# Two parts of the conditioning vectors of a two-block network: row sums on VectorE or products on TensorE

## The chip, the cores and the metric

One NeuronCore of a Trainium2 chip runs the whole program. Its engines each work through their own queue in order: TensorE (PE, with its weight loads PEld), VectorE (DVE), ScalarE (ACT), GpSimd (POOL), and SyncE (SP), which here only issues transfers. The metric is the device time of one execution in microseconds.

## What is computed

Two blocks follow each other on x of 256 x 1024 (float32). The first has two layers: attention with a rotary part, then a state-space mixer, each followed by a feed-forward layer. Each of its four sublayers is modulated by the vector c (1 x 1024):

```python
cs = jax.nn.silu(c)
shift, scale, gate = modulation(cs, w, b)     # split(cs @ w + b, 3), w: 1024 x 3072
h = x * (1.0 + scale) + shift
x = layer_norm(ALPHA * x + (1.0 + gate) * y, g, b)
```

So every sublayer needs three thirds of a vector-matrix product: shift, scale and gate. The second block (recurrent mixer, attention with a bias, gated feed-forward layers) has no modulation and is not touched.

## The kernel before

**Weights.** All weights lie in memory as units of 128 x 1024 float32 (512 KB), in the order in which `plan()` lists them. `_issue` loads them through SP into a ring of seven tiles `raw`. `run` processes units: a weight unit ("w") is split into `wh` (ACT, L464, rounded to fp32r) and `wl` (DVE, L504, the rest) in one of eleven slots, and TensorE then makes three fp32r products for one exact one; a modulation unit ("m") goes to `mod_unit`. A raw tile is loaded anew when the unit in it has been processed, so SP's queue waits on the engines that read the ring.

**Modulation.** `modIT` is third T (0 shift, 1 scale, 2 gate) of sublayer I; it has eight units. A unit holds 128 columns of the weight, turned, so that a partition holds one column. `mod_unit` (L542) multiplies it on DVE by `cs` (silu(c) copied to all partitions) and sums along the row: one `scalar_tensor_tensor` of 128 x 1024 with a sum (L555), which leaves 128 numbers as a column. Shift and scale are wanted as columns (`mcol`), the gate as a full tile: `mod_finish` spreads the column over 128 rows by eight products with the identity and copies them into `GATE` on ACT (L581).

**The stage of the change.** `mla()` is the first attention. After the key and value products it loops over eight heads in `heads`, in an order that a string sets; a letter is a step of the head so many iterations back, a number is `run` for so many units, `q` makes the queries of the next two heads:

```python
HEADS0 = "T2 S0 B0 1 A2 E0 1 N0 q 1"
```

S is the scores (PE; four float32 products and two that add the mask), B the row maxima (DVE), E the exponentials (ACT), N the division by the row sum (DVE reciprocal, ACT), T the turning of the probabilities (PE, copied by ACT, L1095), A the product with the values (PE) and its split (ACT L636, DVE L637). The three `1` take one unit each, so that an iteration also takes one unit of `mla_o`, the output weight, and two modulation units. In `plan()` these are `mod11` (the scale of the first feed-forward layer) and then `mod02` (the gate of the attention itself); the first two units of `mod11` come ahead of the heads. Behind the heads `need_mod("mod02")` calls `mod_finish`, and `boundary("mla_o", ...)` makes the output product, first for the upper 128 rows of x, then for the lower ones. `norm(0)` is the layer norm of the upper half. `make_xt(0)` then modulates the turned upper half and splits it into `XH` (ACT) and `XL` (DVE, L637), and `f_pass` starts the feed-forward product `mlp0.f` with it.

**The tables.** POOL makes four tables of rotations (`rot`) during the heads; they lie in what becomes slots 9 and 10 of the weight ring. `put_tables` (L1440) sends them to memory and marks "tables" as finished; until then `run` can't use these two slots (`self.lent`). In the kernel before it stands directly behind the heads.

Of the kernel before, what the change touches and what calls it, by code (L numbers as in the profile page):

```python
# [11 lines left out]
F32 = mybir.dt.float32  # L12
F32R = mybir.dt.float32r
I32 = mybir.dt.int32
AF = mybir.ActivationFunctionType
# [37 lines left out]

def _mod(i, third):
    return [("m", "mod%d%d" % (i, third), k) for k in range(8)]
# [67 lines left out]
def _unit(inp, kind, tag, k, out):  # L123
# [5 lines left out]

    if kind == "m":  # L130
        i, third = int(tag[3]), int(tag[4])
        nm, l = _MOD[i]
        o = 1024 * third + 128 * k
        out[:] = inp[nm + "_w"][l][:, o:o + 128].T
        return
# [62 lines left out]
def _cols_spec():  # L198
    s = [("dsk", lambda i: i["ssm_d"][0])]
# [44 lines left out]
for _u in UNITS:  # L244
    WPOS.append(WPOS[-1] + (_u[0] == "w"))
    RPOS.append(RPOS[-1] + (_u[0] in "mwx"))
RUNITS = [_j for _j, _u in enumerate(UNITS) if _u[0] in "mwx"]
# [65 lines left out]
class Model:  # L313
    def __init__(self, ctx, tc, ws, cols, rows, x, pos, inv, rel, sp, sbc, sgb, out):
# [33 lines left out]
        self.mhalf = T("mhalf", [128, 4])  # L348
        self.one = T("one", [128, 1])
# [81 lines left out]
    def run(self, look=LOOK, maxn=99, mods=2):  # L431
        n = 0
        while self.nproc < len(UNITS) and n < maxn:
# [4 lines left out]
            if u[0] == "m":  # L438
                if mods == 0 or (self.hold and self.modfin is not None and u[1][4] == '2'):
                    break  # L440
                mods -= 1
# [31 lines left out]
            elif u[0] == "m":  # L473
                self.mod_unit(u, raw)
            elif u[0] == "x":
                self.kept[u] = raw
# [93 lines left out]

    def mod_finish(self):
        if self.modfin is None:
            return
        self.mods.add(self.modfin[0])
        self.modfin = None
        for n in range(2):
            b = self.bank()
            for m in range(4):
                self.mm(b[:, 128 * m:128 * m + 128], self.gcol[:, 4 * n + m:4 * n + m + 1].to_broadcast([128, 128]),
                        self.ident, True, True)  # L580
            self.nc.scalar.activation(self.GATE[:, 512 * n:512 * n + 512], b, func=AF.Copy)  # L581
            self.rel(b)
# [399 lines left out]
    def setup(self):  # L982
# [32 lines left out]
        self.rel(*cb)  # L1015
        self.ssm_decay(spt, pi)
# [93 lines left out]
    def mla(self):  # L1110
# [130 lines left out]
        self.put_tables()  # L1241
# [4 lines left out]
        def norm(h):  # L1246
            if h == 0:
                self.ssm_tables()
                self.halves()
            if h == 1:  # L1250
                self.load_row(self.GR, "ln_mix_g0")
                self.load_row(self.BR, "ln_mix_b0")
            self.ln_part(h, accs[h], ALPHA)
# [850 lines left out]
```

## Time and profile before

| | |
|---|---|
| time, median of 3 runs | 1689.81 us (1685.68 to 1692.23) |
| the profiled execution | 1692.64 us, of it 1690.9 us span |
| mean granted TensorE clock | 0.969 |
| busy over the span | PE 94%, DVE 67%, ACT 50%, POOL 14% |

A span is from the first to the last instruction of the profiled execution, and all times inside it are counted from its start. Busy shares are means over stages that differ: the heads lie between 51 and 124 us, the output product behind them until 148 us. In the views "<-" behind an instruction's idle time names what ended it. PEclk is the granted TensorE clock as a share of 2.4 GHz, so 0.50 is 1.2 GHz. One float32 product appears as two records with two weight loads, one fp32r product as one.

### The profile page before, as it was taken

The numbers are of one execution on the slowest core, as the hardware profiler recorded it, in microseconds if no ns is written. First come the engines' busy times: TensorE is split into PE (matmuls) and PEld (weight loads), VectorE is DVE, ScalarE is ACT, GpSimd is POOL, SyncE is SP. The second block draws the span as 40 slices with busy tenths as digits, with TensorE's granted clock in tenths as the row PEclk, the third lists the DMA queues.
The fourth block names the chain that finished last, engine by engine and source line by source line (L and its number), as shares of the span: only waits on it lengthen the run. The fifth ranks groups of instructions, "written<-read, shape, count | busy, mean of one in ns | idle before, by whom it ended". The sixth has DMA issues, their size and how long they took to land.

```text
span 1690.9 us, 24901 instructions
## 1 busy us (share of the span) xinstructions
PE 1589.7 (94%) x9594; PEld 1400.8 (83%) x9594; DVE 1130.8 (67%) x1568; ACT 838.4 (50%) x1285; POOL 238.5 (14%) x309
## 2 busy tenths in 40 slices
PE   6779999998789999999999889999999999999998
PEld 2558888987778899789997768999899998779997
DVE  7777887779977745767554777555755555775553
ACT  3454567746355655354434745444644444654341
POOL 7990000013523000100000020000000001330000
PEclk8879999998889999999999989999999999999999
DMA  9774788967466566475541547565555663545540
GB/s 367 285 246 157 256 300 295 345 228 294 165 225 244 216 221 206 140 254 198 203 170 47 178 175 260 176 236 174 189 179 189 217 209 103 187 153 203 205 150 26
DMA packets 106586, 349.62 MB, mean 207 GB/s; under 512 B 12385, under 2 KB 22753, under 8 KB 106466
## 3 DMA queue, kind: packets, MB, share of 16 engines
q1 hardware_dynamic: 106466, 348.02, 58.6%
q8 instruction: 75, 1.23, 0.3%
q14 instruction: 45, 0.37, 0.1%
HBM read 338.41 MB, written 9.57 MB: 206 GB/s over the span
## 4 chain that ended last, share of the span: by engine, by line
PE 49%; DVE 4%; ACT 3%; issue 1%; POOL 1%; DMA 0%; DVEq 0%; POOLq 0%; ACTq 0%
PE bank L400 48%; ACT junka L693 1%; DVE wl L504 1%; PE bank L644 1%; ACT wh L464 0%; DMA raw<-in_ws_dram 0%; DVE r L731 0%; ACT r L1870 0%; POOL wl L468 0%; DVE z L1844 0%; ACT z L1871 0%; POOL st L689 0%; DVE z L1300 0%; DVE z L1903 0%; DVE st L1284 0%
## 5 line engine op out<-in xcount | busy, mean ns | idle before, releaser
L504 DVE TENSOR_TENSOR wl<-raw,wh 128x1024 fp32r<-128x1024 f32 x448 | 538.8, 1236 | 161.9 <-ACT wh L464 159.9
L464 ACT ACTIVATE wh<-raw 128x1024 fp32r<-128x1024 f32 x464 | 471.6, 1051 | 246.1 <-PE bank L400 131.8
L400 PE MATMUL bank<-xh,wh 128*128 128x256 f32 x1664 | 469.3, 282 | 0.0
L400 PE MATMUL bank<-xh,wl 128*128 128x256 f32 x1664 | 468.4, 282 | 0.0
L400 PE MATMUL bank<-xl,wh 128*128 128x256 f32 x1664 | 468.3, 281 | 0.0
L400 PEld LDWEIGHTS bank<-xh,wh 128*128 128x128 f32 x1664 | 317.0, 190 | 2.7 <-DVE z L1651 0.2
L400 PEld LDWEIGHTS bank<-xl,wh 128*128 128x128 f32 x1664 | 317.0, 191 | 2.1
L400 PEld LDWEIGHTS bank<-xh,wl 128*128 128x128 f32 x1664 | 317.0, 190 | 0.0
L400 PE MATMUL bank<-wh,hh 128*128 128x512 f32 x736 | 294.2, 400 | 4.7 <-ACT hh L636 4.7
L400 PE MATMUL bank<-wl,hh 128*128 128x512 f32 x736 | 291.0, 395 | 0.0
L400 PE MATMUL bank<-wh,hl 128*128 128x512 f32 x736 | 243.0, 396 | 13.3 <-DVE hl L1914 9.6
L400 PEld LDWEIGHTS bank<-wh,hl 128*128 128x128 f32 x736 | 139.5, 190 | 46.0 <-DVE hl L1914 10.1
L400 PEld LDWEIGHTS bank<-wh,hh 128*128 128x128 f32 x736 | 140.2, 191 | 35.4 <-ACT hh L636 6.3
L400 PEld LDWEIGHTS bank<-wl,hh 128*128 128x128 f32 x736 | 140.2, 191 | 28.5
L555 DVE SCALAR_TENSOR_TENSOR junk<-raw,cs 128x1024 bf16<-128x1024 f32 x96 | 128.9, 1343 | 4.1 <-DMA raw<-in_ws_dram 2.9
L689 POOL TENSOR_TENSOR st<-st,mhalf 128x1 f32<-128x1 f32 (+1 forms) x33 | 22.8, 692 | 759.0 <-DVE st L697 685.9
L400 PE MATMUL bank<-wl,xh 128*128 128x512 f32 x320 | 126.5, 395 | 1.9 <-DVE wl L504 1.0
L400 PE MATMUL bank<-wh,xh 128*128 128x512 f32 x320 | 127.0, 397 | 0.7 <-ACT wh L464 0.7
L637 DVE TENSOR_TENSOR hl<-z,hh 128x512 fp32r<-128x512 f32 x68 | 49.0, 721 | 95.4 <-ACT hh L636 95.4
L400 PE MATMUL bank<-wh,xl 128*128 128x512 f32 x320 | 101.3, 393 | 2.0 <-DVE xl L637 2.0
L636 ACT ACTIVATE hh<-z 128x512 fp32r<-128x512 f32 x68 | 43.0, 632 | 104.3 <-DVE z L929 103.3
L468 POOL TENSOR_TENSOR wl<-raw,wh 128x256 fp32r<-128x256 f32 x64 | 60.7, 980 | 127.5 <-ACT wh L464 127.3
(379 smaller groups left out, 1687.4 us busy)
## 6 DMA issues: line engine op xcount, KB each, us to landing
raw<-in_ws_dram SPq DMA_DIRECT2D x580, 512.0 KB
early<-in_ws_dram SPq DMA_DIRECT2D x10, 512.0 KB
grow<-in_rows_dram SPq DMA_DIRECT2D x9, 512.0 KB
brow<-in_rows_dram SPq DMA_DIRECT2D x6, 512.0 KB
ophh<-ops_d SPq DMA_DIRECT2D x6, 512.0 KB
ophl<-ops_d SPq DMA_DIRECT2D x6, 512.0 KB
gate<-in_rows_dram SPq DMA_DIRECT2D x5, 512.0 KB
tab_d<-rot SPq DMA_DIRECT2D x4, 512.0 KB
```

What stands on the lines that cost most here:

```text
L400: self.nc.tensor.matmul(out, l, r, start=start, stop=stop)
L464: self.nc.scalar.activation(self.Hs[s], raw, func=AF.Copy)
L468: self.nc.gpsimd.tensor_tensor(self.Ls[s][:, w], raw[:, w], self.f32(self.Hs[s])[:, w], op=OP.subtract)
L504: self.nc.vector.tensor_tensor(self.Ls[s], raw, self.f32(self.Hs[s]), op=OP.subtract)
L555: nc.vector.scalar_tensor_tensor(self.junk, raw, 1.0, self.cs, op0=OP.mult, op1=OP.mult, accum_out=total)
L636: self.nc.scalar.activation(hdst, src, func=AF.Copy)
L637: self.nc.vector.tensor_tensor(ldst, src, self.f32(hdst), op=OP.subtract)
L644: self.nc.tensor.transpose(b[:, 128 * j:128 * j + 128], src[:, 128 * k:128 * k + 128], self.ident)
L689: self.nc.gpsimd.tensor_tensor(r, v, self.mhalf[:, 0:n], op=OP.pow)
L693: self.nc.scalar.activation(self.junka[:, 0:512], src, func=AF.Square, scale=scale, accum_out=s[:, n:n + 1])
```

## The change

The units of `mod11` and `mod02` become a kind "g", stored unturned: 128 rows of the weight by 1024 columns. `mod_pass` takes the place of `mod_unit` for them. It holds a column of silu(c) (`cc`, 128 x 8, made in `setup` from a new column of constants) still in TensorE and moves the unit past it in two float32 products of 512 columns; eight units add up in two PSUM banks, which stay taken so long. For `mod11` the still operand is one column, and the result one row; at the last unit ACT copies each half of the row to SBUF, and eight products with a single 1 turn it into a column. For `mod02` the still operand is that column repeated 128 times, so that the result is the full tile; `mod_finish` then adds the bias by eight products with the identity, as many as the spreading took before, and the copy into `GATE` adds 1. `RPOS`, `RUNITS` and `run` count a unit of kind "g" like one of kind "m". The second edit moves `put_tables` from behind the heads into `norm(0)`, that is behind the output product of the upper half.

```diff
@@ -51,8 +51,12 @@
     return [("w", tag, k) for k in range(n)]
 
 
+PEMODS = ("mod11", "mod02",)
+
+
 def _mod(i, third):
-    return [("m", "mod%d%d" % (i, third), k) for k in range(8)]
+    t = "mod%d%d" % (i, third)
+    return [("g" if t in PEMODS else "m", t, k) for k in range(8)]
 
 
 def _ffn_order(tag, nt, first, pair):
...
+    if kind == "g":
+        nm, l = _MOD[int(tag[3])]
+        o = 1024 * int(tag[4])
+        out[:] = inp[nm + "_w"][l][128 * k:128 * k + 128, o:o + 1024]
+        return
...
@@ -568,11 +580,50 @@
                 nc.vector.tensor_scalar(self.gcol, self.gcol, 1.0, None, op0=OP.add)
                 self.modfin = [tag, 3]
 
+
+    def mod_pass(self, u, raw):
+        nc, tag, k = self.nc, u[1], u[2]
+        i, third = int(tag[3]), int(tag[4])
+        wide = third == 2
+        if k == 0:
+            if wide:
+                self.mod_finish()
+            self.gacc[tag] = [self.bank(), self.bank()]
+        acc = self.gacc[tag]
+        c = self.cc[:, k:k + 1]
+        if wide:
+            c = c.to_broadcast([128, 128])
+        for n in range(2):
+            self.mm(acc[n] if wide else acc[n][0:1, :], c, raw[:, 512 * n:512 * n + 512], k == 0, not wide and k == 7)
+        if k < 7:
+            return
+        if wide:
+            self.modfin = [tag, 3]
+            return
+        b = self.bank()
+        for n in range(2):
+            nc.scalar.activation(self.mrow, acc[n][0:1, :], func=AF.Copy)
+            for m in range(4):
+                self.mm(b[:, 4 * n + m:4 * n + m + 1], self.mrow[:, 128 * m:128 * m + 128], self.one[0:1, 0:1], True, True)
+        nc.vector.tensor_tensor(self.mcol[i][third], b[:, 0:8], self.col("modb%d" % i, 8 * third, 8), op=OP.add)
+        self.mods.add(tag)
+        self.rel(b, *self.gacc.pop(tag))
+
     def mod_finish(self):
         if self.modfin is None:
             return
-        self.mods.add(self.modfin[0])
+        tag = self.modfin[0]
+        self.mods.add(tag)
         self.modfin = None
+        if tag in self.gacc:
+            acc = self.gacc.pop(tag)
+            for n in range(2):
+                for m in range(4):
+                    g = self.col("modb%s" % tag[3], 16 + 4 * n + m)
+                    self.mm(acc[n][:, 128 * m:128 * m + 128], g.to_broadcast([128, 128]), self.ident, False, m == 3)
+                self.nc.scalar.activation(self.GATE[:, 512 * n:512 * n + 512], acc[n], func=AF.Identity, bias=self.one)
+            self.rel(*acc)
+            return
         for n in range(2):
             b = self.bank()
             for m in range(4):
@@ -1013,6 +1064,10 @@
             nc.scalar.activation(t, cb[n], func=AF.Tanh)
             V.scalar_tensor_tensor(self.cs[:, 512 * n:512 * n + 512], t, 1.0, cb[n], op0=OP.add, op1=OP.mult)
         self.rel(*cb)
+        cc = self.col("c", 0, 8)
+        nc.scalar.activation(self.cc, cc, func=AF.Tanh, scale=0.5)
+        V.scalar_tensor_tensor(self.cc, self.cc, 1.0, cc, op0=OP.add, op1=OP.mult)
+        V.tensor_scalar(self.cc, self.cc, 0.5, None, op0=OP.mult)
         self.ssm_decay(spt, pi)
         posf = self.posf = self.stat(2)
         V.tensor_copy(posf, posi)
@@ -1238,13 +1293,13 @@
         self.heads(HEADS0, q_pair, qk, None, VV)
         self.lag = self.hold = False
         self.rests()
-        self.put_tables()
         self.need_mod("mod02")
         self.mod_cols(1, "ln_mix_g0", "ln_mix_b0")
         accs = [[self.bank(), self.bank()] for h in range(2)]
 
         def norm(h):
             if h == 0:
+                self.put_tables()
                 self.ssm_tables()
                 self.halves()
             if h == 1:
```

Three places of the queues follow; names are the program's tiles. **TensorE, from the turning of the first head to its product with the values.** `r` holds keys, `z` queries, probabilities and values, `brow` and `maskb` the rotary keys and the mask. Before:

```order
L1094 MATMUL bank_126<-ident,z_98 128x128 x3
L400 MATMUL bank_127<-r_90,z_97 128x256
L400 MATMUL bank_127<-brow,z_97 128x256
L400 LDWEIGHTS identb
L400 MATMUL bank_127<-maskb,identb 128x128
L400 MATMUL bank_127<-r_90,z_97 128x128
L400 MATMUL bank_127<-brow,z_97 128x128
L400 LDWEIGHTS identb
L400 MATMUL bank_127<-maskb,identb 128x128
L400 MATMUL bank_123<-z_98,z_96 128x256
L400 MATMUL bank_123<-z_98,z_96 128x128
```

Now:

```order
L1149 MATMUL bank_125<-ident,z_98 128x128 x3
L410 MATMUL bank_126<-r_90,z_97 128x256
L410 MATMUL bank_126<-brow,z_97 128x256
L410 LDWEIGHTS identb
L410 MATMUL bank_126<-maskb,identb 128x128
L410 MATMUL bank_126<-r_90,z_97 128x128
L410 MATMUL bank_126<-brow,z_97 128x128
L410 LDWEIGHTS identb
L410 MATMUL bank_126<-maskb,identb 128x128
L410 MATMUL bank_130<-raw_67,cc 1x512
L410 MATMUL bank_131<-raw_67,cc 1x512
L410 MATMUL bank_127<-z_98,z_96 128x256
```

Between the scores of the third head and the first head's product with the values stands a unit of `mod11`, two products of 512 columns; such a pair stands at each place where `run` takes a modulation unit.

**VectorE, in the same heads.** L1284 (now L1339) is the row maximum, L1227 to L1229 (L1282 to L1284) the rotary part of the queries. Before:

```order
L504 TENSOR_TENSOR wl_37_572<-raw_69,wh_37_571 128x1024
L555 SCALAR_TENSOR_TENSOR junk,msum<-raw_63,cs 128x1024
L1284 TENSOR_REDUCE st<-bank_130 128x1 x2
L555 SCALAR_TENSOR_TENSOR junk,msum<-raw_64,cs 128x1024
L1295 RECIPROCAL st<-st 128x2
L504 TENSOR_TENSOR wl_40_606<-raw_65,wh_40_605 128x1024
L555 SCALAR_TENSOR_TENSOR junk,msum<-raw_66,cs 128x1024
L1284 TENSOR_REDUCE st<-bank_127 128x1 x2
L555 SCALAR_TENSOR_TENSOR junk,msum<-raw_67,cs 128x1024
L637 TENSOR_TENSOR hl_87<-bank_123,hh_86 128x256
```

Now:

```order
L516 TENSOR_TENSOR wl_37_579<-raw_69,wh_37_578 128x1024
L1339 TENSOR_REDUCE st<-bank_129 128x1 x2
L1350 RECIPROCAL st<-st 128x2
L516 TENSOR_TENSOR wl_40_615<-raw_65,wh_40_614 128x1024
L1339 TENSOR_REDUCE st<-bank_126 128x1 x2
L688 TENSOR_TENSOR hl_87<-bank_127,hh_86 128x256
L1350 RECIPROCAL st<-st 128x2
L1282 TENSOR_TENSOR z_97<-bank_124,brow 128x256
L1283 TENSOR_TENSOR z_97<-bank_124,brow 128x256
L1284 TENSOR_TENSOR z_97<-z_97 128x256
```

The row sums (L555) are gone, and everything else keeps its order.

**VectorE, around the layer norm of the upper half.** `wl_59` and `wl_60` are the splits of `mlp0.f` 1 and 2, which go into slots 9 and 10; L705 to L720 (L756 to L771) are the norm, `scol`, `bcol` and `xl` belong to `make_xt(0)`. Before:

```order
L504 TENSOR_TENSOR wl_59_905<-raw_63,wh_59_904 128x1024
L504 TENSOR_TENSOR wl_60_910<-raw_64,wh_60_909 128x1024
L1413 TENSOR_TENSOR spp<-ident 128x32
L1414 TENSOR_TENSOR spp<-spp,ident 128x32
L1415 TENSOR_TENSOR spp<-spp,ident 128x32
L705 TENSOR_TENSOR r_90<-bank_125,gate 128x512
L706 SCALAR_TENSOR_TENSOR r_90<-x_88,r_90 128x512
L707 BN_STATS st<-r_90 128x6
```

Now:

```order
L762 TENSOR_SCALAR st<-st 128x1
L771 TENSOR_SCALAR r_90<-r_90,st 128x512 x2
L516 TENSOR_TENSOR wl_59_960<-raw_63,wh_59_959 128x1024
L516 TENSOR_TENSOR wl_60_965<-raw_64,wh_60_964 128x1024
L516 TENSOR_TENSOR wl_37_579<-raw_65,wh_37_578 128x1024
L516 TENSOR_TENSOR wl_40_615<-raw_66,wh_40_614 128x1024
L516 TENSOR_TENSOR wl_43_647<-raw_67,wh_43_646 128x1024
L516 TENSOR_TENSOR wl_46_702<-raw_68,wh_46_701 128x1024
L728 TENSOR_SCALAR z_98<-bank_126,scol,bcol 128x128 x4
L688 TENSOR_TENSOR xl<-z_98,xh 128x4x128 x2
```

The two splits stood ahead of the norm and now stand behind it, ahead of four more splits and of `make_xt(0)`. ACT's halves of the two splits move behind the copy in `ssm_tables`, which `norm(0)` calls. On SP the four transfers of the tables keep their place behind the load of `mlp0.f` 7; two later loads now follow the eight small transfers that `norm(0)` issues, where they stood ahead of them.

## Rows read from the trace of the kernel before

**Rows 1.** Busy time by stretch; heads, half-clock stretch, output product.
```profile
core 0: us, PE busy (x) PEld busy (x) DVE busy (x) ACT busy (x) POOL busy (x), PEclk, DMA share, GB/s
51.50:112.00 60.50, 47.36 (x193) 33.53 (x191) 49.34 (x84) 29.47 (x73) 57.56 (x67) 0.85 0.68 238
...
108.00:113.30 5.30, 5.30 (x17) 3.37 (x16) 4.86 (x14) 4.04 (x10) 5.14 (x11) 0.50 0.88 315
...
124.40:147.80 23.40, 23.40 (x110) 19.19 (x109) 14.24 (x24) 9.39 (x14) 1.78 (x10) 1.00 0.42 139
```

**Rows 2.** Groups by line, 46 to 121 us, VectorE: the row sums.
```profile
L555 DVE SCALAR_TENSOR_TENSOR junk<-raw,cs 128x1024 bf16<-128x1024 f32 x22 | 32.9, 1495 | 0.2
```

**Rows 3.** TensorE's waits, 51.5 to 112 us: total us, times, longest.
```profile
PE bank L400 <- ACT z L1095: 9.9, 3, 5.2
PE bank L400 <- DVE z L1229: 3.2, 1, 3.2
```

**Rows 4.** Timeline of TensorE: start, us, engine, line, operation; values, queries, first scores.
```profile
51.48 3.60 PE L400 MATMUL bank<-early,gate 128*128 128x512 f32 x8
54.91 3.62 PE L400 MATMUL bank<-gate,early 128*128 128x256 f32 x16
58.36 0.59 PE L400 MATMUL bank<-r,z 128*128 128x256 f32 x2
```

**Rows 5.** Timeline of TensorE, one head at the full clock.
```profile
82.72 0.60 PE L400 MATMUL bank<-r,z 128*128 128x256 f32 x2
...
84.80 0.87 PE L400 MATMUL bank<-z,z 128*128 128x256 f32 x4
85.51 0.49 PE L1094 MATMUL bank<-ident,z 128*128 128x128 f32 x3
85.84 0.38 PE L400 MATMUL bank<-r,z 128*128 128x256 f32 x1
```

**Rows 6.** Timeline, the wait inside the first head's scores.
```profile
60.90 0.41 DVE L1227 TENSOR_TENSOR z<-bank,brow 128x256 f32<-128x256 f32 x1
...
62.21 0.70 PE L400 MATMUL bank<-brow,z 64*128 64x256 f32 x2 [3.25 <-DVE z L1229]
```

**Rows 7.** Timeline, from the last scores to the output product.
```profile
111.70 1.27 DVE L555 SCALAR_TENSOR_TENSOR junk<-raw,cs 128x1024 bf16<-128x1024 f32 x1
...
111.89 1.60 PE L400 MATMUL bank<-z,z 128*128 128x256 f32 x4
...
113.30 0.61 DVE L1284 TENSOR_REDUCE st<-bank 128x1 f32<-128x256 f32 x2
...
121.23 3.49 PE L400 MATMUL bank<-ident,gcol 128*128 128x128 f32 x16
...
123.18 0.60 ACT L581 ACTIVATE gate<-bank 128x512 f32<-128x512 f32 x1 [1.32 <-PE bank L400]
```

**Rows 8.** Timeline of VectorE, from the second moved split to `xl`.
```profile
128.33 1.23 DVE L504 TENSOR_TENSOR wl<-raw,wh 128x1024 fp32r<-128x1024 f32 x1 [0.72 <-DMA tab_d<-rot]
...
141.84 4.63 DVE L504 TENSOR_TENSOR wl<-raw,wh 128x1024 fp32r<-128x1024 f32 x4
...
147.66 1.48 DVE L637 TENSOR_TENSOR xl<-z,xh 128x512 fp32r<-128x512 f32 x2
```

**Rows 9.** Timeline of TensorE, start of the feed-forward product.
```profile
147.79 0.39 PE L400 MATMUL bank<-wh,xh 128*128 128x512 f32 x1
148.02 0.39 PE L400 MATMUL bank<-wl,xh 128*128 128x512 f32 x1
...
148.70 0.62 PE L400 MATMUL bank<-wh,xl 128*128 128x512 f32 x2
```

**Rows 10.** Timeline, VectorE in the first sublayer: an early row sum.
```profile
12.65 1.23 DVE L555 SCALAR_TENSOR_TENSOR junk<-raw,cs 128x1024 bf16<-128x1024 f32 x1 [0.64 <-DMA raw<-in_ws_dram]
```

**Rows 11.** TensorE's waits, 124 to 420 us, the two longest.
```profile
PE bank L400 <- POOL z L1667: 6.1, 1, 6.1
PE bank L400 <- DVE hl L637: 3.6, 1, 3.6
```

More of the change, by code (lines that the diff above doesn't have):

```diff
@@ L198, in _cols_spec @@
 def _cols_spec():
-    s = [("dsk", lambda i: i["ssm_d"][0])]
+    s = [("dsk", lambda i: i["ssm_d"][0]), ("c", lambda i: i["c"][0])]
     for m, (nm, l) in _MOD.items():
@@ L245 @@
     WPOS.append(WPOS[-1] + (_u[0] == "w"))
-    RPOS.append(RPOS[-1] + (_u[0] in "mwx"))
-RUNITS = [_j for _j, _u in enumerate(UNITS) if _u[0] in "mwx"]
+    RPOS.append(RPOS[-1] + (_u[0] in "gmwx"))
+RUNITS = [_j for _j, _u in enumerate(UNITS) if _u[0] in "gmwx"]
 SPARE = [(WPOS[UNITS.index(("w", "ssm_in", 7)) + 1] + _k) % RING for _k in SPARES]
@@ L348, in __init__ @@
         self.mhalf = T("mhalf", [128, 4])
+        self.cc, self.mrow, self.gacc = T("cc", [128, 8]), self.junk[0:1, :].bitcast(F32), {}
         self.one = T("one", [128, 1])
@@ L437, in run @@
                 break
-            if u[0] == "m":
+            if u[0] in "gm":
                 if mods == 0 or (self.hold and self.modfin is not None and u[1][4] == '2'):
@@ L474, in run @@
                 self.mod_unit(u, raw)
+            elif u[0] == "g":
+                self.mod_pass(u, raw)
             elif u[0] == "x":
```

## The prediction, made before the changed kernel ran

> **What bounds the kernel now.** I read the stretch of the heads first, then the queues inside it. From 51.5 us (the products of the values) to 112.0 us (the end of the eighth head's scores) are 60.5 us; VectorE is busy for 49.3 of them and TensorE for 47.4, at a granted clock of 0.85 of 2.4 GHz [rows 1]. So neither is full. VectorE's largest piece is the row sums: 22 of 1.50 us between 46 and 121 us [rows 2], of which 16 are the units of `mod11` and `mod02`. TensorE is idle for 60.50 - 47.36 = 13.1 us, and these gaps end with ACT's copies of turned probabilities (9.9 us) and with the rotary part of the first queries (3.2 us) [rows 3]; both stand behind row sums in VectorE's queue, directly or through the maxima and reciprocals. Behind the heads TensorE has no gap: 23.40 of 23.40 us at the full clock [rows 1]. Whatever delays the start of the output product therefore delays what follows it.
>
> What does TensorE's work in those 60.5 us take at the full clock? A head's scores run from 82.72 to 84.80, 2.08 us; its product with the values to 85.51, 0.71 us; a turning to 85.84, 0.33 us [rows 5]. The values' four products are eight records from 51.48 to 54.91, 3.43 us; a pair of query heads runs from 54.91 to 58.36, 3.45 us [rows 4]. Eight scores, six turnings, five products with values, four query pairs and the values: 16.6 + 2.0 + 3.6 + 13.8 + 3.4 = 39.4 us. The free time is 60.5 - 39.4 = 21.1 us, 13.1 of it gaps and 8.0 the slower clock.
>
> **The change part by part.** *Row sums.* VectorE loses 16 x 1.50 = 24 us [rows 2]. It then has some 25 us of work in 60, so it no longer paces the heads.
>
> *Products.* TensorE gains 16 units x 2 = 32 float32 products of 512 columns. The values' products have this size and type: four in 3.43 us, 0.857 each, as two records of 0.43 [rows 4]. 32 x 0.857 = 27.4 us. I take the same for a still operand of one column, since the moving columns are as many. All 32 come ahead of the last scores in the order.
>
> *Turning `mod11`'s row into a column.* Two copies on ACT, 0.60 us each like the copy into the gate, and eight small float32 products, 16 records, at 3.49 / 16 = 0.22 us like those with the identity [rows 7]: 1.2 + 3.5 = 4.7 us. TensorE waits for each copy, and the second copy for the first four products (one buffer). Bounds: 1.2 (copies alone) and 6 (copies held up in ACT's queue by as much again).
>
> *What takes it up.* Of the 21.1 us free, 1.3 stay: the rotary part of the first queries takes VectorE from 60.90 to 62.21 [rows 6], and it can't begin before the queries are made. The rest, 19.8, takes up passes: they stand just where TensorE waited for ACT, and with a full queue the clock should be granted. If the clock stays at its present mean, only 11.8 are there. So the last scores end 27.4 + 4.7 - 19.8 = 12.3 us later.
>
> *From the last scores to the output product.* In this tail a row sum (111.70, 1.27 us) delays the last maximum to 113.30 [rows 7]; without it the maximum comes up to 1.2 earlier, though ACT still waits for the sixth head's product. I take 1.0 off; bounds 0 and 3 (if the tail also runs at the full clock). The bias products are as many as the spreading products before, and count as nothing.
>
> *Tables.* The transfers keep their place on SP. What moves are the splits of `mlp0.f` 1 and 2. Before, VectorE made them in idle time ahead of the norm, the second at 128.33 after 0.72 us of waiting for the tables, off TensorE's path [rows 8]. Now they stand between the norm and `make_xt(0)`, where four splits already run back to back from 141.84 for 4.63 us, 1.16 each [rows 8]: 2.3 us more. The first half of `xl` is there at 147.66 + 0.74 = 148.40 [rows 8], and TensorE's fifth product of the feed-forward layer wants it at 148.70 [rows 9]. 0.3 us of slack against 2.3: TensorE stands still for 2.0 us. Bounds 0 and 2.4. The lower half of the norm, behind on VectorE, is late by as much as TensorE is, so nothing is added there. The two loads that now stand behind the small transfers on SP wait for the splits anyway.
>
> *Setup.* `cc` costs one activation and two VectorE operations of 128 x 8 ahead of the first row sums. The third row sum waits 0.64 us for its weights [rows 10], which covers them; without that cover they cost at most those 0.6 us.
>
> **Sum:** 12.3 - 1.0 + 2.0 = +13.3 us. The profiled execution (1692.6) would become 1705.9; it lies 2.8 us over the median, so I add to the median: 1689.8 + 13.3 = **1703.1 us**. With the bounds the sum goes from 27.4 + 1.2 - 19.8 - 3 + 0 = 5.8 to 27.4 + 6 - 11.8 + 2.4 = 24.0: 1695.6 to 1713.8.
>
> **A rule against the trace.** The values' row shows 0.43 us for a record of 512 float32 columns at the full clock [rows 4]. The Trainium skill (TensorE: Matmul & The Clock Gate, Back-to-back issue gap) gives N / 2.4 + 2.5 ns, 0.216 us for 512 columns. By it, taken once per product, the 32 products would be an estimated 6.9 us, TensorE would have room for them, and the sum would be an estimated -7.2 us in place of +13.3. The trace does not agree: a float32 product is two records of twice that time. The skill's page FP8 and Floating Point Precision (Matmul Precision, TensorE Precision Notes) counts four passes for true float32, which gives an estimated 0.864, and with that the trace agrees.
>
> **The rivals.** *Cheap passes (the other side).* If a pass past a still column costs one record at the rate of fp32r, 0.23 us (147.79 to 148.02 [rows 9]), the products take 32 x 0.23 = 7.4 us. Then 7.4 + 4.7 - 19.8 = -7.7, and the sum is -7.7 - 1.0 + 2.0 = -6.7: 1683.1, not slower. It decides at (19.8 - 4.7) / 32 = 0.47 us per product. Against it: the operands are float32, as in the values' row. Chance 0.10.
>
> *The clock.* If TensorE's stop at the turning lets the clock fall, the 32 us of work between it and the last scores (eight units, five scores and so on) run partly at 1.2 GHz. For it: from 108 to 113.3 TensorE is busy throughout and is granted 0.50 [rows 1]. A third of that work at half speed is +10.7: 1713.8. Against it: long passes leave few gaps. Chance 0.15.
>
> *Given back later.* Behind the output product TensorE waits once 6.1 us for POOL and once 3.6 us for VectorE [rows 11]. If those producers don't start later, 9.7 come back: +3.6, 1693.4. Against it: they stand in order behind the norm on VectorE. Chance 0.17.
>
> **How the numbers follow.** The forecast has 0.58. A difference under 0.5%, 8.4 us, can't be told from none here: the borders are 1681.4 and 1698.3. Slower: the clock's 0.15 and 0.50 of the forecast, 0.65. Same: the forecast's lower end 0.08, given back 0.17, and 0.06 of the cheap passes, 0.31. Faster: their other 0.04. The range, 1692 to 1716, takes in the bounds of the sum, given back and most of the clock; it leaves out the cheap passes and a little at the top.
>
> **What would show it.** Right: passes of 0.86 us per product, TensorE with few gaps from 51 us to the last scores, these near 124 us, the output product near 136 us; VectorE with gaps of several us in the heads; a wait of some 2 us of TensorE for `xl` in the feed-forward product. Wrong: passes of 0.23 us, the output product before 124 us, a granted clock under 0.8 in the heads, or long waits for POOL and VectorE gone in the later stages.

## The result, and the profile after

The change takes 1708.9 us in the median of 6 runs (1706.8 to 1715.1), the kernel before 1690.5 (6 runs, 1685.7 to 1692.2): **1.0107 times as long, 95% interval 1.0093 to 1.0120**, or 16 to 20 us more. The forecast of 1703.1 and its +13.3 had the sign, and the mechanism of its largest term; the median, 18.4 us over that of the kernel before, lies inside the range. The profiled execution takes 1706.8 us, 14.2 more than that of the kernel before; its span is 1705.0 against 1690.9.

The stretch of the heads and the stretch that held the output product, by engine, in the change (busy time, granted clock in the column PEclk; it answers to [rows 1]):

```profile
core 0: us, PE busy (x) PEld busy (x) DVE busy (x) ACT busy (x) POOL busy (x), PEclk, DMA share, GB/s
51.50:112.00 60.50, 58.82 (x213) 31.84 (x210) 21.08 (x43) 22.31 (x53) 50.09 (x117) 0.94 0.53 192
124.40:147.80 23.40, 19.80 (x90) 16.22 (x89) 6.35 (x15) 7.86 (x18) 0.00 (x0) 0.85 0.51 183
```

VectorE fell from 49.3 to 21.1 us and TensorE rose from 47.4 to 58.8 of 60.5: the bound of the stretch has moved from VectorE's queue to TensorE. Its waits from 51.5 to 126 us, in total, times and longest, against 13.1 us before [rows 3]:

```profile
PE bank L410 <- DVE z L1284: 0.9, 1, 0.9
PE bank L410 <- ACT junk L605: 0.7, 1, 0.7
```

Neither wait is for a PSUM bank, so no wait in the profile comes from the two banks that stay taken for eight units.

TensorE's timeline in the same stretch (start, us, engine, line, operation, its shapes, how many records; it answers to [rows 4, 7]):

```profile
50.51 1.88 PE L410 MATMUL bank<-raw,cc 128*1 128x512 f32 x4
52.32 3.70 PE L410 MATMUL bank<-early,gate 128*128 128x512 f32 x8
55.95 1.88 PE L410 MATMUL bank<-raw,cc 128*1 128x512 f32 x4
...
88.03 1.05 PE L410 MATMUL bank<-one,junk 1*128 1x1 f32 x8
89.81 1.05 PE L410 MATMUL bank<-one,junk 1*128 1x1 f32 x8 [0.74 <-ACT junk L605]
90.79 0.55 PE L1149 MATMUL bank<-ident,z 128*128 128x128 f32 x3
...
93.89 3.73 PE L410 MATMUL bank<-raw,cc 128*128 128x512 f32 x4
97.41 1.49 PE L410 MATMUL bank<-z,z 128*128 128x256 f32 x4
...
108.93 1.88 PE L410 MATMUL bank<-raw,cc 128*128 128x512 f32 x4
110.65 0.49 PE L1149 MATMUL bank<-ident,z 128*128 128x128 f32 x3
...
126.15 0.87 PE L410 MATMUL bank<-z,z 128*128 128x256 f32 x4
```

One unit of `mod02` is four records from 108.93 to 110.65, so 0.86 us per product, the price taken from the values' row. The Trainium skill (FP8 and Floating Point Precision, Matmul Precision, TensorE Precision Notes) counts four passes for true float32, by the prediction's working an estimated 0.864 us. The change agrees. Three things were not in the working. A unit of `mod11`, with one still column, takes 1.81 us (50.51 to 52.32); the values behind it take 3.63 (52.32 to 55.95) instead of 3.43 [rows 4]. And one unit behind the turning takes 3.52 us (93.89 to 97.41). The windows of 2 us there give the clock:

```profile
90.00:92.00 2.00, 2.00 (x14) 1.65 (x14) 0.17 (x1) 0.49 (x1) 1.61 (x8) 1.00 0.75 254
92.00:94.00 2.00, 2.00 (x9) 1.23 (x8) 0.00 (x0) 0.00 (x0) 2.00 (x10) 0.59 0.64 229
94.00:96.00 2.00, 2.00 (x4) 0.97 (x4) 0.62 (x2) 0.00 (x0) 2.00 (x11) 0.50 0.01 2
96.00:98.00 2.00, 2.00 (x4) 0.88 (x4) 0.00 (x0) 0.00 (x0) 1.91 (x10) 0.50 0.00 0
98.00:100.00 2.00, 2.00 (x7) 1.32 (x6) 0.42 (x1) 1.07 (x5) 1.91 (x10) 0.71 0.69 217
```

TensorE is busy in every one of them, yet from about 92.3 to 99.2 us the clock is 1.2 GHz. Just ahead lie a stop of 0.74 us for the second copy of the row (the first was there in time) and the 16 one-column records of the turning.

The feed-forward product of the change, its first, fourth, fifth and sixth kind of record (they answer to [rows 9]):

```profile
160.40 0.39 PE L410 MATMUL bank<-wh,xh 128*128 128x512 f32 x1
...
161.08 0.39 PE L410 MATMUL bank<-wl,xh 128*128 128x512 f32 x1
163.45 0.76 PE L410 MATMUL bank<-wh,xl 128*128 128x512 f32 x2 [1.98 <-DVE xl L688]
164.02 0.61 PE L410 MATMUL bank<-wh,xh 128*128 128x512 f32 x1
164.43 0.63 PE L410 MATMUL bank<-wl,xh 128*128 128x512 f32 x1
```

The wait for `xl` is there, 1.98 us against 2.0 in the sum. VectorE's row ahead of it shows why; six splits stand where four stood [rows 8]:

```profile
154.62 6.90 DVE L516 TENSOR_TENSOR wl<-raw,wh 128x1024 fp32r<-128x1024 f32 x6
```

Behind the wait the records stand 0.43 us apart instead of 0.23: the granted clock is 0.57 from 164 to 168 us. The change's delay along the program, from the same rows in both traces (us):

| place | before | after | delay |
|---|---|---|---|
| heads begin (values before, a pass now) | 51.48 | 50.51 | -1.0 |
| values, first record | 51.48 | 52.32 | 0.8 |
| last scores end | 111.89 | 126.15 | 14.3 |
| output product begins | 124.47 | 137.35 | 12.9 |
| feed-forward product begins | 147.79 | 160.40 | 12.6 |
| its fifth product (`xl`) | 148.70 | 163.45 | 14.8 |
| up product begins | 170.79 | 186.95 | 16.2 |
| first product behind POOL's `z` | 408.98 | 422.99 | 14.0 |
| a row of VectorE in the second layer | 1060.64 | 1072.98 | 12.3 |
| end of the span | 1690.9 | 1705.0 | 14.1 |

The change's execution began the heads 1.0 us earlier. From their beginning to the last scores it took 75.6 us instead of 60.4: the heads themselves cost 15.2, and the last scores are 14.3 late. The tail gave 1.4 back, the tables took 3.6. Between the up product and the row in the second layer 3.9 came back, 2.2 of it ahead of POOL's `z`. What follows from about 1000 us on, 1.8 us more, is in no term of the sum.

### The profile page after: what moved, and what is told of

The parts are those of the page before. It is cut to its first block, busy times and chain, and to the rows that moved or that the text cites. A ratio compares the mean times of both kernels' runs of the same rounds, so it can differ in the third digit from the quotient of the medians.

```text
span 1705.0 us, 25028 instructions
## 1 busy us (share of the span) xinstructions
PE 1613.0 (95%) x9674; PEld 1412.5 (83%) x9674; DVE 1106.4 (65%) x1536; ACT 838.8 (49%) x1288; POOL 219.1 (13%) x309
## 4 chain that ended last, share of the span: by engine, by line
PE 49%; DVE 4%; ACT 3%; issue 1%; POOL 0%; DMA 0%; DVEq 0%; POOLq 0%; ACTq 0%
PE bank L410 48%; ACT junka L744 1%; ACT wh L474 1%; PE bank L695 1%; DVE wl L516 0%; DMA raw<-in_ws_dram 0%; ACT r L1925 0%; POOL wl L478 0%; DVE z L1899 0%; DVE r L782 0%; ACT z L1926 0%; DVE z L1355 0%; DVE z L1958 0%; DVE st L1339 0%; ACT z L1923 0%
## 5 line engine op out<-in xcount | busy, mean ns | idle before, releaser
L410 PE MATMUL bank<-wh,hl 128*128 128x512 f32 x736 | 241.2, 393 | 14.8 <-DVE hl L1969 9.6
L688 DVE TENSOR_TENSOR hl<-z,hh 128x512 fp32r<-128x512 f32 x68 | 49.3, 725 | 94.3 <-ACT hh L687 94.3
L567 DVE SCALAR_TENSOR_TENSOR junk<-raw,cs 128x1024 bf16<-128x1024 f32 x80 | 105.1, 1314 | 4.0 <-DMA raw<-in_ws_dram 2.6
L478 POOL TENSOR_TENSOR wl<-raw,wh 128x256 fp32r<-128x256 f32 x64 | 60.5, 980 | 128.1 <-ACT wh L474 127.9
```

The source lines that it names most:

```text
L410: self.nc.tensor.matmul(out, l, r, start=start, stop=stop)
L478: self.nc.gpsimd.tensor_tensor(self.Ls[s][:, w], raw[:, w], self.f32(self.Hs[s])[:, w], op=OP.subtract)
L567: nc.vector.scalar_tensor_tensor(self.junk, raw, 1.0, self.cs, op0=OP.mult, op1=OP.mult, accum_out=total)
L688: self.nc.vector.tensor_tensor(ldst, src, self.f32(hdst), op=OP.subtract)
```

## The experiments

Each was timed in rounds against the kernel before on the same chip, whose medians there were 1692.1, 1691.6, 1692.6 and 1692.4 us in the four groups below. In the tables below, "delay in the heads" is that of the first VectorE row of the upper half's norm, just behind its output product (135.6 us in the kernel before), in the profiled execution of each. It is one execution each, and not a fine measure: the kernel before with its tiles shifted (`e9_before_shifted`, below), whose heads do the same work, stands at -2.6.

### Taking the change apart

`e1_passes_only` and `e2_tables_only` part the two halves of the change:

```diff
         self.rests()
+        self.put_tables()
         self.need_mod("mod02")
...
             if h == 0:
-                self.put_tables()
                 self.ssm_tables()
```

(the first as shown, from the change; the second the other way round, from the kernel before). `e3_only_mod02` and `e4_only_mod11` are the first with one line more:

```diff
-PEMODS = ("mod11", "mod02",)
+PEMODS = ("mod02",)
```

and `("mod11",)`. What was expected:

> The change, with the storing of the tables put back ahead of the norm, where the kernel before has it. Theory A (the tables' term stands apart): TensorE's wait of 2.0 us for xl in the feed-forward product and the half clock behind it go away; in the trace of the change this place went from 12.6 to 16.4 us behind the kernel before, so the product ends 3.8 us earlier, and the time is 2.0 to 3.8 us under the change's 1708.9: 1705 to 1707. Theory B (given back later): what the tables cost is waited for anyway further on, and the time stays at 1708.9 within 1.5 us.

> The kernel before with nothing changed but the storing of the tables, which goes into the norm. Theory A: TensorE waits 2.0 us for xl near 149 us, and the granted clock may fall behind it; 2.0 to 3.8 us over the 1690.5 of the kernel before: 1692.5 to 1694.3. Theory B: the wait is there, but a later wait shrinks by as much, and the time stays at 1690.5 within 1.5 us.

> Only the gate mod02 by passes on TensorE; mod11 as row sums on VectorE, the tables ahead of the norm. Theory A (TensorE's free time of the stretch takes passes up until it is full): 16 products of 0.86 us are 13.7 us; the kernel before has 6.9 us of gaps behind 88 us and loses some 5.5 us to the half clock there, 12.4 together, so the last scores move by 1.3 and the tail gives 1.0 back: 1690 to 1692. Theory B (each pass costs what it costs in the change, half of the whole): half of 14.5, +7 us, 1697 to 1698.

> Only mod11 by passes on TensorE, with the turning of its row; the gate mod02 as row sums, the tables ahead of the norm. Theory A: 13.7 us of products and 2.8 us of turning; up to 88 us the kernel before has 1.9 + 3.0 us of gaps that can be filled and loses some 4.4 us to the half clock, 9.3 together, and a part of the 5.2 us gap behind 88 us: the last scores move by 2 to 7 us, and the time is 1692 to 1697. Theory B (half of the whole): +7 us, 1697 to 1698.

| run | median us | ratio to the kernel before (95%) | delay in the heads |
|---|---|---|---|
| the change | 1708.9 | 1.0107 (1.0093 to 1.0120) | 12.8 |
| passes only | 1707.8 | 1.0103 (1.0084 to 1.0122) | 13.2 |
| tables only | 1695.7 | 1.0019 (1.0006 to 1.0032) | 0.2 |
| only `mod02` | 1696.6 | 1.0024 (1.0012 to 1.0036) | 3.2 |
| only `mod11` | 1698.9 | 1.0046 (1.0028 to 1.0064) | 8.4 |

Nearly all of the loss is that of the passes. The tables alone cost 1 to 5 us; in that trace the wait is there again, with slow records behind it:

```profile
150.88 0.74 PE L400 MATMUL bank<-wh,xl 128*128 128x512 f32 x2 [1.86 <-DVE xl L637]
...
152.84 1.06 PE L400 MATMUL bank<-wh,xl 128*128 128x512 f32 x2
```

That is theory A, with the fall of the clock. On top of the passes, though, the tables can't be seen in the time (theory B): in the trace of the passes alone this place runs without a wait, at 13.0 us of delay where the change has 16.5, but near 320 us TensorE stands at about 14.2 in both. The passes alone lose 1.4 us further on (its waits for `hl` between 189 and 279 us sum to 5.9 us, those of the kernel before in the same piece of the program to 3.6), and the change, after rising to 17.7 at 240 us, gets 2 back. Which of the later waits grows or shrinks differs from run to run; I can't say that the tables' cost is always returned.

Of the halves, `mod11` has the larger delay in its trace, 8.4 against 3.2 us, but the intervals of the times overlap, and in its execution the clock was 0.50 for some 13 us behind the turning (from 91.5 us on), which costs 6 to 7 us. For `mod02` neither theory holds: 3.2 us where a full use of the free time would have given some 0.3. For `mod11` the ranges lay too close to be told apart by the time.

### What a product costs

`e5_bf16_passes` (tables ahead of the norm) reads the upper half of each weight, past a column of silu(c) that is rounded to bf16 into a small tile of its own:

```diff
-            self.mm(..., c, raw[:, 512 * n:512 * n + 512], ...)
+            self.mm(..., c, raw.bitcast(mybir.dt.bfloat16)[:, 1024 * n + 1:1024 * n + 1024:2], ...)
```

`e8_few_columns` keeps float32 and moves fewer columns; `e6_no_turning` is the whole change without the row's turning, so that the scale of the feed-forward layer (the expectation says shift) lacks its product:

```diff
-            self.mm(..., c, raw[:, 512 * n:512 * n + 512], ...)
+            e = 512 if k in (0, 7) else 128
+            self.mm(...[:, 0:e], c, raw[:, 512 * n:512 * n + e], ...)
```

```diff
-        for n in range(2):
-            nc.scalar.activation(self.mrow, acc[n][0:1, :], func=AF.Copy)
-            for m in range(4):
-                self.mm(b[:, 4 * n + m:4 * n + m + 1], self.mrow[...], self.one[0:1, 0:1], True, True)
+        self.mm(b[:, 0:8], self.ident, self.ident[:, 0:8], True, True)
```

> The passes alone (tables ahead of the norm), with each weight cut to the bf16 number in its upper half and silu(c) rounded to bf16, so that a product is one record. Theory A (the price of a float32 product decides, the cheap rival of the prediction): 32 products of about 0.23 us are 7.4 instead of 27.4; TensorE no longer fills the stretch, VectorE still has its 24 us less, and the last scores come 5 to 8 us ahead of the kernel before: 5 to 9 us faster than it. Theory B (with room again, TensorE waits between the passes and works at the half clock): passes of 0.45 us or more in the profile, and the time within 3 us of the kernel before.

> The change without the turning of the row of mod11: the two copies and the eight small products are left out, and one small product with the identity stands in their place, so the shift of the modulation holds the bias and wrong numbers. Theory A (the stop at the turning also lets the granted clock fall to one half from 92 to 99 us, which costs 3.6 us): 2.8 and 3.6 us come off, and the time is 1701 to 1704, at a granted clock near 1.0 from 88 to 100 us. Theory B (the clock falls there for another reason): only 2.6 us come off, 1705.5 to 1707.5.

> The passes alone (tables ahead of the norm); six of the eight units of each third move only 128 of each 512 columns, so three quarters of their products are left out. The products cost 8 x 0.86 + 24 x 0.22 = 12.1 us instead of 27.4. Theory A (TensorE's time bounds the stretch, one to one, until its free time is reached): 15.3 us come off the passes' 1707.8, within 2 us of the kernel before. Theory B (what is taken off comes back as waits and half clock): 4 us or more over the kernel before. Theory C (the wait for the passes was only part, VectorE's relief is worth more): 4 us or more under the kernel before.

| run | median us | ratio to the kernel before (95%) | delay in the heads |
|---|---|---|---|
| bf16 passes | 1694.6 | 1.0023 (1.0010 to 1.0036) | -1.6 |
| no turning | 1705.9 | 1.0085 (1.0067 to 1.0104) | 9.2 |
| few columns | 1691.9 | 1.0003 (0.9990 to 1.0015) | -3.5 |

*Few columns:* with 15.3 us of products gone, 15.9 us of the median go (17 by the ratios): theory A, nearly one to one. TensorE's own work is what the change lost by; and with passes of less than half the cost nothing is left of the loss. In the traces the clock helps: that of the passes alone has half clock behind the turning, as the change has, that of few columns has not.

*bf16 passes:* the cheap rival's price is right, its time is not. A unit with 128 still columns takes 0.45 us (94.32 to 94.77), 0.23 per product. The heads end only 1.6 us earlier instead of 5 to 8, and this execution had begun them 2.1 us early (a row at 46.1 us of the kernel before), so they won nothing. Of theory B the half clock and the time came (3.0 us over the kernel before), but not its price per product, and TensorE's waits in the heads are only 3.0 us. The clock took a large part of the gain. Two records and two windows of that trace:

```profile
94.32 0.61 PE L411 MATMUL bank<-raw,ccb 128*128 128x512 bf16 x2
94.77 0.81 PE L411 MATMUL bank<-z,z 128*128 128x256 f32 x4
...
60.00:70.00 10.00, 9.17 (x33) 5.46 (x34) 3.23 (x8) 4.31 (x9) 8.71 (x29) 0.83 0.45 168
82.00:92.00 10.00, 9.77 (x33) 6.92 (x34) 2.29 (x6) 2.17 (x8) 9.32 (x14) 0.53 0.44 160
```

TensorE is busy for 9.8 of the 10 us from 82 on, at 0.53: busy at half speed. Ahead of it the turning stops TensorE, here twice:

```profile
80.45 1.05 PE L411 MATMUL bank<-one,junk 1*128 1x1 f32 x8 [0.45 <-ACT junk L606]
82.23 1.56 PE L411 MATMUL bank<-one,junk 1*128 1x1 f32 x8 [0.74 <-ACT junk L606]
```

This trace loses another 3.8 us from about 1000 us on, which the section on the places of the tiles takes up.

*No turning:* the window from 88 to 100 us, which held the half clock in the change, and the two records between which that piece of the heads lies:

```profile
88.00:100.00 12.00, 12.00 (x49) 6.27 (x48) 4.95 (x11) 4.37 (x12) 11.37 (x35) 1.00 0.39 132
...
90.78 0.53 PE L1146 MATMUL bank<-ident,z 128*128 128x128 f32 x3
...
122.86 0.87 PE L410 MATMUL bank<-z,z 128*128 128x256 f32 x4
```

Full clock. From the end of the turning's place to the product behind the last scores it takes 32.1 us (90.78 to 122.86), the change 35.4 (90.79 to 126.15): 3.3 us were the clock. The turning itself cost 2.8 us; whether it also made the clock fall is not shown. The trace answers to theory A, but the time, 1705.9, lies in the range of theory B (between the two, if the 1.1 us are taken off by which the kernel before was slower in these rounds), and this profiled execution began the heads 2.5 us later than that of the change. And a run of the next group speaks against a fixed link. `e10_after_old_places` has the same passes and the same turning, with the same stop:

```profile
92.15 1.05 PE L410 MATMUL bank<-one,junk 1*128 1x1 f32 x8 [0.74 <-ACT junk L605]
93.13 0.55 PE L1150 MATMUL bank<-ident,z 128*128 128x128 f32 x3
...
125.23 0.87 PE L410 MATMUL bank<-z,z 128*128 128x256 f32 x4
...
90.00:102.00 12.00, 11.26 (x55) 7.04 (x53) 3.76 (x7) 4.47 (x12) 11.36 (x44) 1.00 0.39 132
```

The clock stays at 1.00, and the piece behind the turning takes 32.1 us (93.13 to 125.23), as long as without a turning. In the run with few columns, too, the clock is 1.00 from 51 to 110 us behind a stop of 0.7 us. Of the six traces with such a stop four show the fall (the change, passes only, only `mod11`, bf16 passes), and none of the four in which TensorE isn't stopped there.

### The places of the tiles

The last 1.8 us of the delay table lie behind 1000 us, among the large products. The groups by line, 1000 to 1690 us (total us, mean ns of one), in the kernel before and in the change:

```profile
L400 PE MATMUL bank<-xh,wl 128*128 128x256 f32 x928 | 260.9, 281 | 0.0
...
L400 PE MATMUL bank<-wh,hh 128*128 128x512 f32 x297 | 117.3, 395 | 0.7 <-ACT hh L636 0.7
```

```profile
L410 PE MATMUL bank<-xh,wl 128*128 128x256 f32 x928 | 262.6, 283 | 0.0
...
L410 PE MATMUL bank<-wh,hh 128*128 128x512 f32 x302 | 118.5, 392 | 0.8 <-ACT hh L687 0.8
```

The same instructions on the same shapes. `e9_before_shifted` gives the kernel before nothing but the change's two small allocations; `e10_after_old_places` takes them out of the change:

```diff
-    s = [("dsk", lambda i: i["ssm_d"][0])]
+    s = [("dsk", lambda i: i["ssm_d"][0]), ("c", lambda i: i["c"][0])]
...
+        self.cc = T("cc", [128, 8])
```

```diff
-        self.st = T("st", [128, 144])
+        self.st = T("st", [128, 136])
...
-        self.cc, self.mrow, self.gacc = T("cc", [128, 8]), self.junk[0:1, :].bitcast(F32), {}
+        self.mrow, self.gacc = self.junk[0:1, :].bitcast(F32), {}
...
         cc = self.col("c", 0, 8)
...
+        self.cc = cc
```

`e11_bf16_spread` joins the old places to the bf16 passes, with the tables ahead of the norm, and spreads the turning: one copy at the last unit of `mod11`, four products and the other copy at the next unit, four products at the one behind it.

> The kernel before, with its computation as it was, and the two small allocations of the change: eight more columns in the tile of constants and a tile of 128 x 8, which move every SBUF tile that is allocated behind them by 64 bytes per partition. Between 1000 and 1690 us the records of the large products last otherwise in the change than before: 283 against 281 ns where 256 columns move, 392 against 395 ns where 512 move, and the delay grows there by 2 us. Theory A (the places of the tiles do this): this kernel shows 283 and 392 ns, and takes 1.5 to 4 us more than the kernel before. Theory B (it follows from the passes or from the later start): 281 and 395 ns, and the time of the kernel before within 1.2 us.

> The change, with silu(c) made in its own columns of the constants and 8 fewer columns in the ring of statistics, so that the tiles behind stand where the kernel before has them. Theory A (the places of the tiles add to the change's time): 281 and 395 ns between 1000 and 1690 us, and 1.5 to 4 us off the change: 12 to 16 us over the kernel before, where the change lies 18. Theory B: 283 and 392 ns and 17 to 19 us over the kernel before.

> The bf16 passes with the tables ahead of the norm, the tiles in their old places, and the turning of mod11's row spread over three units, so that TensorE has other work while ACT copies. Theory A (the fall to half clock from 82 to 93 us in the bf16 run came from the stop at the turning): the granted clock stays near 1.0 behind the turning, the last scores come 5 to 8 us ahead of the kernel before, and the time is 3 to 8 us under it. Theory B (the clock falls for lack of work): half clock for some 10 us between 62 and 112 us all the same, and within 2 us of the kernel before.

The rows of the kernel before, shifted, and of the change in the old places:

```profile
L401 PE MATMUL bank<-xh,wl 128*128 128x256 f32 x928 | 262.6, 283 | 0.0
...
L401 PE MATMUL bank<-wh,hh 128*128 128x512 f32 x296 | 116.1, 392 | 0.8 <-ACT hh L637 0.8
```

```profile
L410 PE MATMUL bank<-xh,wl 128*128 128x256 f32 x928 | 260.8, 281 | 0.0
...
L410 PE MATMUL bank<-wh,hh 128*128 128x512 f32 x304 | 120.1, 395 | 0.7 <-ACT hh L687 0.7
```

The durations follow the places and not the passes: theory A for the records. In time it is little. The shifted kernel is at 1693.9 us, 1.0012 (0.9998 to 1.0026); its trace loses 3.0 us between 1000 and 1640 us. The change in the old places is at 1707.3, 1.0086 (1.0069 to 1.0102), and loses 0.7 us there, but its interval overlaps that of the change, and its heads, without the half clock, took 3.2 us less than those of the change (72.4 against 75.6 from the first pass to the last scores), so the places aren't all that differs. A cost of 1 to 3 us fits all of it; the times alone don't show it. The traces do, taken together: from TensorE's records near 1000 us to the last one the delay against the kernel before grows by 1.8 to 3.4 us in each of the seven kernels with shifted tiles (2.0 in the change) and by 3.8 in the bf16 passes, and changes by -0.4 to +0.7 in the five others with the old places.

The spread bf16 passes take 1684.1 us, **0.9951 (0.9937 to 0.9964): 6 to 11 us under the kernel before**, with 9.5 us won in the heads. Where the other bf16 run had 0.53, the clock is full:

```profile
82.00:92.00 10.00, 9.93 (x56) 7.90 (x57) 4.14 (x11) 6.88 (x19) 9.60 (x10) 1.00 0.78 287
```

The forecast of theory A came, a little more than its 8 us of time and of heads, and the kernel beats both others, at the price of the lower 16 bits of the weights of these two thirds and of silu(c). That the stop at the turning was the cause isn't shown by it: the tiles moved too, and the clock is seen in one execution of each.

### The one still column

Slower records stood in every run with passes of one still column, in float32 and in bf16, in old places and new; in `e3_only_mod02`, which has none, the values took 3.43 us. `e12_f32_all_wide` and `e13_bf16_all_wide` spread silu(c) over 128 still columns for `mod11` too, the one in float32, the other in bf16, both with spread turning, tables ahead of the norm and old places:

```diff
-        if wide:
-            c = c.to_broadcast([128, 128])
+        c = c.to_broadcast([128, 128])
...
-            self.mm(acc[n] if wide else acc[n][0:1, :], c, ...)
+            self.mm(acc[n], c, ...)
```

> The change in float32 with its side costs taken away: tables ahead of the norm, the tiles in their old places, the turning of mod11's row spread over three units, and the column of silu(c) spread to 128 still columns for mod11 too (its row is then read from one partition of the sums). Wherever mod11 goes by passes with one still column, the values' eight records took 3.63 us, in runs without such passes 3.43, and two products of a pass 1.81 instead of 1.72. Theory A (the one still column slows the records around it): 3.43 and 1.72 from the first pass on; what is left is the prediction's main term, 27.4 of products and 2.1 of small products less 19.8 taken up and 1.0 of the tail, +8.7: 8 to 11 us over the kernel before. Theory B (the slower records have another cause): 3.63 and 1.81 stay, and 10 to 13 us over it.

> The spread bf16 passes with 128 still columns for mod11 too. Theory A: the values' records 3.43 us again, 0.5 to 1.5 us less than the 8.5 us by which the spread bf16 passes were under the kernel before: 9 to 10 us under it. Theory B: 3.63 us stay, 7.5 to 9 us under it.

The start of the heads in the float32 run, which answers to the rows from 50.51 us above:

```profile
51.47 1.91 PE L410 MATMUL bank<-raw,cols 128*128 128x512 f32 x4
53.22 3.60 PE L410 MATMUL bank<-early,gate 128*128 128x512 f32 x8
56.65 1.88 PE L410 MATMUL bank<-raw,cols 128*128 128x512 f32 x4
58.37 3.62 PE L410 MATMUL bank<-gate,early 128*128 128x256 f32 x16
```

3.43 us for the values (53.22 to 56.65) and 1.72 for a unit (56.65 to 58.37): theory A. This run takes 1701.5 us, 1.0065 (1.0049 to 1.0081), so 8 to 14 us over the kernel before; in its trace the last scores end 9.9 us late (121.75) and the first row of the norm 9.6. The bf16 run takes 1685.1 us, 0.9956 (0.9940 to 0.9973): its values take 3.43 us too, but nothing was won over the spread passes before, because this execution waited 1.5 us for the rotary part and ran at a clock of 0.83 from 60 to 70 us (1.0 us and 1.00 in the spread run before). On its time neither theory is shown.

## Why the prediction was right, and where its terms were off

*What bounds the kernel.* Right. The relief of VectorE (24 us by the sum, 28 in the stretch) was worth only the gaps that it had caused, and TensorE was filled by what replaced it.

*Products.* Right: 0.86 us with 128 still columns, and 15.3 us of products taken away took 15.9 us off the time. The one place where it was off: "I take the same for a still operand of one column". Eight such units took 14.4 us instead of 13.7, and the values and queries between them 0.6 more, some 1.3 us together (`e12_f32_all_wide` shows that the one column was the cause).

*Turning.* 2.8 us (88.03 to 90.79) against 4.7: the first copy was waited for nowhere, the second 0.74 us, and the 16 records took 2.0.

*What takes it up.* "With a full queue the clock should be granted" is the step that failed in part: the queue was full, and the clock fell all the same behind the turning, for 3.3 us. The rival of the clock named such a fall; it came with a third of its price of 10.7, and its cause, the stop at the turning, is open, since the same stop left the clock at 1.00 in `e10_after_old_places` and `e8_few_columns`. In sum the heads took 15.2 us more instead of 12.3: 1.9 less for the turning, 1.3 more for the still column, 3.3 more for the clock leave 15.0; TensorE's wait for the rotary part was 0.9 and not 1.3, which leaves 14.6, and 0.6 are in no term. The early start of this execution (1.0) brings the last scores to 14.3.

*Main term by itself.* With the side costs gone, the float32 run should show the products (27.4) and the small products of the turning (2.0) less the 19.8 taken up, and it did: 9.6 by the working, 9.9 at the last scores. That it agrees to 0.3 is partly luck. The free time is read from one execution, in which the heads took 60.3 us from the first record of the values to the last of the scores; in the shifted kernel before, which does the same work there, they took 54.9 (52.03 to 106.88), and the same working would have left some 14 us of room instead of 19.8.

*Tail.* 1.4 us instead of 1.0.

*Tables.* The wait was 1.98 us against 2.0. The step left out what came behind the wait, half clock for another 1.6 us; by itself the move costs 1 to 5 us. Together with the passes it came to nothing that the times can show.

*Setup.* Costed at nothing for its time. What it moved in SBUF was not thought of; with it go the 1.8 us behind 1000 us.

*The rivals.* "Given back later" didn't happen in the form named: TensorE still waits 6.17 us for POOL's `z`, and the wait for `hl` grew from 3.6 to 5.2. What did come back is 3.9 us, from 16.2 of delay at the up product to 12.3 in the second layer; 2 us of it at 285 us, where a wait of 1.8 us for `hh` is gone. Cheap passes had the price right, but as an experiment they came out slower than the kernel before, until the turning was spread and the tiles stood in their old places; 0.23 us per product alone was not enough.

*Size.* The traces differ by 14.2 us, close to the forecast of 13.3, but partly by luck: 2.9 more in the heads, 1.6 more behind the wait for `xl` and 1.8 more at the end stand against 1.0 of early start, 0.4 of the tail and the 3.9 that came back. The medians differ by 18.4. Only one execution of each kernel is profiled, that of the change the shortest of its times and that of the kernel before longer than all its own, so the other 4 us lie in executions without a trace, and no row can tell what they are made of.

## What to carry to other kernels

Work that leaves a full engine should go to one whose free time, at the full clock, is larger than the new price: compare the price per product with the free time per product, type first (float32 0.86 us, bf16 0.23 for the same columns). Then put no stop into the stretch just filled, since a copy that TensorE waits for costs its own time (0.74 us here), and in four of six traces the clock fell behind it: spread such a step over the units that follow. A small new tile can be put into space that is there, so that nothing behind it moves. And a difference of a few us in one stage needs more than one execution of each kernel.

## What the runs showed of the hardware

- A product with one still column slows the float32 products around it at an unchanged granted clock: 512 moving columns 1.81 instead of 1.72 us per two products, the values 3.63 instead of 3.43, and 128 still columns cure it. It shows in all eight traces with such passes, two of them in bf16, and in neither of the two that made them wide, nor in the four that have none.
- Moving the tiles by 64 bytes per partition changes the mean of the large products' records, 281 to 283 ns where 256 columns move and 395 to 392 where 512 do, to the same digit in every kernel with these places (seven shifted, six not; the first bf16 run, whose new tiles take 80 bytes, shows 282 and 395). From about 1000 us to the end the shifted seven lose 1.8 to 3.4 us against the kernel before, the others at most 0.7.
- The clock can be at 1.2 GHz while TensorE is busy without a gap: 7 us in the change behind a turning with one stop of 0.74 us, some 10 us in the bf16 run behind one with two. The same turning with the same stop left it at 2.4 GHz in `e10_after_old_places` and `e8_few_columns`. The Trainium skill (TensorE: Matmul & The Clock Gate, What's actually happening) says that the clock follows how busy the array has been recently; what decided between these traces no run shows.
- Executions begin the heads up to 2 us earlier or later (the row at 46.12 us in the kernel before, -2.1 to +1.3 us among the kernels), behind a stretch in which the DMA engines are busy for 0.95 of the time. The heads themselves took 60.3 us in the trace of the kernel before and 54.9 in that of the shifted one, at a granted clock of 0.85 and 0.89 from 51.5 to 112 us. A difference of traces in one later stage is better read from a row at its start, and even so not to less than some us.
